# Attention scores over all 128 rows of TensorE, in smaller steps, in a hybrid decoder layer

## The chip, the cores and the metric

One core of a Trainium2 chip runs the whole layer. The metric is the device time of one execution in microseconds (us). The core has a matrix engine, TensorE (PE in the profile; PEld is its load of weights, which runs beside it), a vector engine (DVE), a scalar engine (ACT), GpSimd (POOL), and a queue SP that only issues DMA transfers. TensorE's clock has two levels, 1.2 and 2.4 GHz; the profile gives the granted clock as a share of 2.4 GHz.

## The reference, cut to what matters

One sequence of 512 tokens of width 1024, float32. The layer runs two kinds of attention on one projection, adds both through one output matrix, and then runs a feed-forward part and a gated embedding.

```
h = rmsnorm(x);  mq, mk, mv, rq, rk, rv, rg = split(h @ w_in)
# MoBA: 8 heads of 64; with 2 blocks of 256 keys and top-3 every earlier block is taken
s = (mq @ mk.T) * 64**-0.5 - slope[head] * distance      # causal
moba = softmax(s) @ mv
ret = groupnorm(chunkwise_retention(rq, rk, rv)) * silu(rg)   # 4 heads of 128
x = x + concat(moba, ret) @ w_out
h = rmsnorm(x);  x = x + (gelu(conv(h @ w_up)) * (h @ w_gate)) @ w_down
x = x + (p @ w_ple) * sigmoid(rmsnorm(x) @ w_ple_gate);  return rmsnorm(x)
```

## The kernel before

Every matrix product is made in split precision: an operand is kept as a rounded part `hi` and a rest `lo`, and `mm3` (line 91) issues three matmuls, hi by hi, hi by lo and lo by hi. ACT makes `hi`, DVE subtracts to get `lo` (`split`, line 78). Weights arrive as tiles `wr` on SP's queue, ACT makes `wh` (line 152), and DVE or POOL makes `wl` (line 154; POOL for the projection and the output matrix). There are two buffers `wr` and three each of `wh` and `wl`. SBUF tiles of 2 KB per partition come from one heap, and TensorE's results from eight PSUM banks.

The stages are: projections and retention, then the stretch from about 158 to 273 us in which MoBA is worked off, then the sum of attention outputs with the next norm, then up, gate and down products, then the gated embedding.

In the MoBA stretch two heads (one pair `g`, the two halves of a 128-row feature tile) and one block `b` of 256 queries make a round i, eight in all. `moba_scores` (line 455) makes the scores `ms` of two query tiles and both heads. Its first matmul of a score (L466) uses the 64 rows of one head: query hi by key hi. The second (L468) uses 128 rows and makes both cross products in one: the query tile holds hi in one head's half and lo in the other half, and the key tile `mk` holds lo and hi the other way round. The softmax of a score is a custom DVE operation that adds the bias and finds the smallest (`ml`, L447), an exponential with its sum on ACT (`me`, `mt`, L450), a reciprocal (`mi`, L452) and a scaling (L453) on DVE. One round later `moba_turn` (line 483) transposes the probabilities on TensorE (`mp`) and splits them into `corner`, or `mph` and `mpl` (L497, L498). Another round later `moba_values` (line 501) multiplies them with the values (`mo`) and splits the result into `mxh` and `mxl`.

Between these pieces stand fills (line 621): the last five feature projections (`pj`, 24 matmuls of 512 columns each, lines 93 to 95), the first half of the output product (`ou`, 12 each) and the products of the embedding (`pw`, 6 each, with `wph` and `pTh`, `pTl` as operands). A round is: all scores of the round, a fill, the values, the transposes, a fill.

A query projection is split into four half pieces (two ACT copies on L369, two DVE subtractions on L370). A key projection is split into one whole `mkh`, two half subtractions (L378) and two transfers on SP that put a half of `mkh` into the other half of the tile (L377). Queries come ahead of keys in the list `feature_tiles` (line 167).

After attention, for each of eight feature rows: `x` (L671) adds the output product, `h2h` and `h2l` (L88) split the next product's operand, and `squares` (line 652) squares the row on ACT and adds it to `sqs` on DVE. `next_norm` (line 663) does the split and the squares of a row together.

TensorE's order is the program's, pinned by hand (line 823). The order on the other engines comes from a scheduler, which takes due times from its own model.

## Time and profile before

| what | value |
|---|---|
| median of 3 runs | 707.64 us (707.6 to 708.22) |
| the profiled execution | 708.11 us, of which the trace's span is 706.3 us |
| TensorE busy | 688.7 us of the span, mean granted clock 0.991 |
| DVE, ACT, POOL busy | 445.6, 284.8 and 126.9 us |

The profiled execution lies 0.47 us above the median. TensorE is busy nearly all the time, so the time lost is to be looked for in single waits, which the view of waits lists by the engine that waited, what it wanted to do, and what released it. A matmul's listed duration overlaps with the next one, so what a matmul costs is read from the distance of two starts.

### The profile page before, as it was taken

What the parts mean: (1) busy time and instruction counts of PE and PEld (TensorE: products, weight loads), DVE (VectorE), ACT (ScalarE), POOL (GpSimd) and SP (SyncE); (2) the same over time, 40 slices, a digit from 0 to 9 for tenths busy, and PEclk for the clock granted to TensorE, in tenths of its full rate; (3) what the DMA queues carried; (4) which work ended last, traced back from release to release, by engine and by line L of the source; (5) the groups of instructions that cost most, each with busy time, mean ns of one, the idle gap of its engine ahead of it and who ended that gap; (6) DMA issues with size and microseconds to landing.
All of it is one profiled execution on the core that took longest, in us unless ns stands there. A gap on an engine that the chain in (4) does not pass through costs nothing.

```text
span 706.3 us, 8382 instructions
## 1 busy us (share of the span) xinstructions
PE 688.7 (98%) x3200; PEld 568.4 (80%) x3200; DVE 445.6 (63%) x792; ACT 284.8 (40%) x463; POOL 126.9 (18%) x100
## 2 busy tenths in 40 slices
PE   8999999999989999999999999999999999999995
PEld 6888888887767888788888888888888888888884
DVE  4675677777868885676556653324555665466496
ACT  4534543335555584544334332112343343354311
POOL 6135342345535111000000000000000000000146
PEclk9999999999989999999999999999999999999998
DMA  8245224325222101133133122233332311445003
GB/s 265 101 115 143 66 75 113 81 67 172 56 79 75 60 2 59 61 120 119 60 119 106 59 89 90 89 107 117 119 94 85 120 54 59 134 135 186 1 0 120
DMA packets 70525, 66.65 MB, mean 94 GB/s; under 512 B 1890, under 2 KB 62166, under 8 KB 70486
## 3 DMA queue, kind: packets, MB, share of 16 engines
q1 hardware_dynamic: 70310, 65.86, 30.2%
q8 instruction: 25, 0.41, 0.2%
q10 hardware_dynamic: 144, 0.26, 0.1%
q14 instruction: 14, 0.11, 0.0%
q0 software_dynamic: 32, 0.00, 0.0%
HBM read 62.97 MB, written 2.10 MB: 92 GB/s over the span
## 4 chain that ended last, share of the span: by engine, by line
PE 88%; DVE 7%; issue 2%; ACT 2%; DMA 0%; DVEq 0%; POOL 0%; ACTq 0%; POOLq 0%
PE gate L93 6%; PE gate L95 6%; PE dn L94 6%; PE dn L95 6%; PE gate L94 6%; PE dn L93 6%; PE up L94 5%; PE up L95 5%; PE up L93 5%; PE pj L93 5%; PE pj L94 5%; PE pj L95 5%; PE pg L94 1%; PE pg L95 1%; PE pg L93 1%
## 5 line engine op out<-in xcount | busy, mean ns | idle before, releaser
L152 ACT ACTIVATE wh<-wr 128x1024 fp32r<-128x1024 f32 (+2 forms) x108 | 105.3, 978 | 202.9 <-PE dn L94 66.4
L154 DVE TENSOR_TENSOR wl<-wr,wh 128x1024 fp32r<-128x1024 f32 (+2 forms) x78 | 84.7, 1086 | 47.8 <-ACT wh L152 47.7
L154 POOL TENSOR_TENSOR wl<-wr,wh 128x1024 fp32r<-128x1024 f32 x30 | 73.1, 2437 | 160.0 <-ACT wh L152 151.2
L94 PE MATMUL up<-h2l,wh 128*128 128x512 f32 x176 | 68.6, 390 | 1.5 <-DVE h2l L88 1.5
L93 PE MATMUL gate<-h2h,wh 128*128 128x512 f32 x176 | 68.7, 390 | 0.0
L95 PE MATMUL up<-h2h,wl 128*128 128x512 f32 x176 | 68.5, 389 | 0.0
L95 PE MATMUL gate<-h2h,wl 128*128 128x512 f32 x176 | 68.5, 389 | 0.0
L94 PE MATMUL gate<-h2l,wh 128*128 128x512 f32 x176 | 68.5, 389 | 0.0
L93 PE MATMUL up<-h2h,wh 128*128 128x512 f32 x176 | 68.5, 389 | 0.0
L93 PE MATMUL dn<-ach,wh 128*128 128x512 f32 x176 | 68.5, 389 | 0.0
L94 PE MATMUL dn<-acl,wh 128*128 128x512 f32 x176 | 68.5, 389 | 0.0
L95 PE MATMUL dn<-ach,wl 128*128 128x512 f32 x176 | 68.5, 389 | 0.0
L93 PE MATMUL pj<-h1h,wh 128*128 128x512 f32 x160 | 64.1, 401 | 2.9 <-DVE mpl L498 2.8
L94 PE MATMUL pj<-h1l,wh 128*128 128x512 f32 x160 | 63.1, 394 | 0.0
L95 PE MATMUL pj<-h1h,wl 128*128 128x512 f32 x160 | 62.9, 393 | 0.0
L691 POOL MEMSET u<- 128x2 f32 x22 | 2.2, 102 | 292.4 <-DVE c L698 292.4
L702 DVE TENSOR_TENSOR ga<-gate,r2b 128x512 f32<-128x512 f32 x22 | 15.2, 691 | 41.4 <-PE gate L95 41.4
L94 PEld LDWEIGHTS up<-h2l,wh 128*128 128x128 f32 x176 | 33.0, 188 | 8.8 <-DVE h2l L88 1.9
L692 DVE TENSOR_TENSOR u<-up,r2b 128x512 f32<-128x512 f32 x22 | 15.1, 692 | 39.3 <-PE up L95 39.3
L93 PEld LDWEIGHTS dn<-ach,wh 128*128 128x128 f32 x176 | 33.0, 188 | 6.9
L94 PEld LDWEIGHTS dn<-acl,wh 128*128 128x128 f32 x176 | 33.0, 188 | 6.9
L94 PEld LDWEIGHTS gate<-h2l,wh 128*128 128x128 f32 x176 | 33.0, 188 | 6.9
(233 smaller groups left out, 1421.9 us busy)
## 6 DMA issues: line engine op xcount, KB each, us to landing
wr<-in_w_up_dram SPq DMA_DIRECT2D x11, 1024.0 KB, 5.4
wr<-in_w_gate_dram SPq DMA_DIRECT2D x11, 1024.0 KB, 5.3
wr<-in_w_in_dram SPq DMA_DIRECT2D x20, 512.0 KB, 4.0
wr<-in_w_down_dram SPq DMA_DIRECT2D x8, 768.0 KB, 4.3
wr<-in_w_down_dram SPq DMA_DIRECT2D x8, 640.0 KB, 4.0
wr<-in_w_ple_gate_dram SPq DMA_DIRECT2D x4, 1024.0 KB, 5.6
wr<-in_w_out_dram SPq DMA_DIRECT2D x3, 1024.0 KB, 5.0
xn<-in_x_dram SPq DMA_DIRECT2D x8, 256.0 KB, 5.8
```

The lines of the kernel that those rows point to most:

```text
L93: nc.tensor.matmul(acc, a[0], b[0], start=first, stop=False)
L94: nc.tensor.matmul(acc, a[0], b[1], start=False, stop=False)
L95: nc.tensor.matmul(acc, a[1], b[0], start=False, stop=last)
L152: nc.scalar.activation(hi, part, AF.Copy)
L154: (nc.gpsimd if aside else nc.vector).tensor_tensor(lo, part, f(hi), op=ALU.subtract)
L691: nc.gpsimd.memset(u[:, 0:2], 0.0)
L692: nc.vector.tensor_tensor(u[:, 2:], up, r2b, op=ALU.mult)
L702: nc.vector.tensor_tensor(ga, gate, r2b, op=ALU.mult)
```

## The change

For each pair of heads the queries are split whole (one ACT copy, one DVE subtraction), and four transfers on SP stack hi over lo for each head in a tile `mq2`. The keys are split whole as well, and eight transfers build four tiles `mk2`: hi over hi and lo over lo for each head. A score is then two matmuls over 128 rows, the stack by hi, hi and the stack by lo, lo. This adds the product of lo by lo, which was not computed before. The number of score matmuls stays 64. The key projections come ahead of the query projections. A round's scores are cut into two steps, one query tile each, and its transposes into two, one head each, and the fills are spread over three places in a round. Last, the squares of all eight rows of `x` come after the last row's split, not with each row.

```diff
-    feature_tiles += [(n, h) for h in range(HR) for n in ("mq", "mk")]
+    feature_tiles += [(n, h) for h in range(HR) for n in ("mk", "mq")]
...
-            two = [h2k("mq", F32R) for _ in range(2)]
+            both = split(t, "mq")
+            two = [h2k("mq2", F32R) for _ in range(2)]
             for e in range(2):
-                nc.scalar.activation(two[e][HALF[e]], t[HALF[e]], AF.Copy)
-                nc.vector.tensor_tensor(two[e][HALF[1 - e]], t[HALF[e]], f(two[e][HALF[e]]), op=ALU.subtract)
+                for part, half in zip(both, HALF):
+                    nc.sync.dma_start(f(two[e][half]), f(part[HALF[e]]))
...
-            hi = hi_of(t, "mk")
-            two = [h2k("mk", F32R) for _ in range(2)]
-            for e in range(2):
-                nc.sync.dma_start(f(two[e][HALF[1 - e]]), f(hi[HALF[e]]))
-                nc.vector.tensor_tensor(two[e][HALF[e]], t[HALF[e]], f(hi[HALF[e]]), op=ALU.subtract)
-            qs[name, i] = (hi, two)
+            both = split(t, "mk")
+            two = [[h2k("mk2", F32R) for _ in range(2)] for _ in range(2)]
+            for part, tiles in zip(both, two):
+                for e in range(2):
+                    for half in HALF:
+                        nc.sync.dma_start(f(tiles[e][half]), f(part[HALF[e]]))
+            qs[name, i] = two
...
-        for qt in (2 * b, 2 * b + 1):
+        for qt in (2 * b + step,):
...
             for e in range(2):
-                nc.tensor.matmul(ss[e][:, :wide], q[e][HALF[e], own], kh[HALF[e], :wide], start=True, stop=False)
-            for e in range(2):
-                nc.tensor.matmul(ss[e][:, :wide], q[e][:, own], kx[e][:, :wide], start=False, stop=True)
+                nc.tensor.matmul(ss[e][:, :wide], q[e][:, own], kh[e][:, :wide], start=True, stop=False)
+                nc.tensor.matmul(ss[e][:, :wide], q[e][:, own], kl[e][:, :wide], start=False, stop=True)
...
-    fills = []
-    for i in range(5):
-        fills += [[big[i]], mid[i - 1:i]]
-    fills += [[mid[4], few[0]], [mid[5], few[1]], [mid[6], few[2]], [mid[7], few[3]], few[4:5], few[5:6], few[6:7],
-              few[7:8], [], []]
+    fills = [[big[0]], [], []]
+    for i in range(1, 5):
+        fills += [[big[i]], mid[i - 1:i], []]
+    fills += [[mid[4], few[0]], [mid[5]], [few[1]], [mid[6], few[2]], [mid[7]], [few[3]], [few[4]], [few[5]], [],
+              [few[6]], [few[7]], [], [], [], []]
...
-        if i < HM:
-            moba_scores(i // 2, i % 2)
-        for go in fills[2 * i]:
-            go()
+        for step in range(2):
+            if i < HM:
+                moba_scores(i // 2, i % 2, step)
+            for go in fills[3 * i + step] if step == 0 else []:
+                go()
...
-        if 1 <= i <= HM:
-            moba_turn((i - 1) // 2, (i - 1) % 2)
-        for go in fills[2 * i + 1]:
-            go()
+        for e in range(2):
+            if 1 <= i <= HM:
+                moba_turn((i - 1) // 2, (i - 1) % 2, e)
+            for go in fills[3 * i + 1 + e]:
+                go()
...
-        return squares(x1[dt], sums)
...
-            sums = next_norm(dt - 1)
-    sums = next_norm(ND - 1)
+            next_norm(dt - 1)
+    next_norm(ND - 1)
+    for t in x1:
+        sums = squares(t, sums)
```

What this does to the order is shown at three places around the first scores. On TensorE, before, the first row below is the end of projection 15 (queries of the second pair), the eight `ms` rows are the first round's scores, and `pj_16` is the key projection that follows:

```order
L95 MATMUL pj_15_1543<-h1h_8_342,wl_19_1470 128x512
L466 MATMUL ms_1_1594<-mkh_1_1500,mq_1_1435 128x256
L466 MATMUL ms_2_1595<-mkh_1_1500,mq_2_1436 128x256
L468 MATMUL ms_1_1594<-mk_1_1502,mq_1_1435 128x256
L468 MATMUL ms_2_1595<-mk_2_1503,mq_2_1436 128x256
L466 MATMUL ms_3_1614<-mkh_1_1500,mq_1_1435 128x256
L466 MATMUL ms_4_1615<-mkh_1_1500,mq_2_1436 128x256
L468 MATMUL ms_3_1614<-mk_1_1502,mq_1_1435 128x256
L468 MATMUL ms_4_1615<-mk_2_1503,mq_2_1436 128x256
L93 MATMUL pj_16_1642<-h1h_1_147,wh_20_1539 128x512
```

On TensorE now (`pj_15` is now the keys and `pj_16` the queries of the second pair):

```order
L95 MATMUL pj_15_1555<-h1h_8_342,wl_19_1480 128x512
L470 MATMUL ms_1_1616<-mk2_1_1439,mq2_1_1514 128x256
L471 MATMUL ms_1_1616<-mk2_3_1441,mq2_1_1514 128x256
L470 MATMUL ms_2_1617<-mk2_2_1440,mq2_2_1515 128x256
L471 MATMUL ms_2_1617<-mk2_4_1442,mq2_2_1515 128x256
L93 MATMUL pj_16_1640<-h1h_1_147,wh_20_1551 128x512
```

The first score pair now reads four tiles `mk2` and two tiles `mq2` that transfers have put together, and the second query tile's scores (`ms_3`, `ms_4`) have moved behind the 24 matmuls of `pj_16`.

On DVE, before, at the same place (`pt_14` takes the key projection out of PSUM, `rrv` to `rry` and `rrt` are the small steps of a reciprocal square root for retention, `mk` is the keys' lo half, `mxl` the lo part of the last retention head but one):

```order
L434 TENSOR_TENSOR rt2_3_1458<-rrow_3_1459,rt1_3_1251 128x512
L82 TENSOR_TENSOR mxl_3_1467<-rt2_3_1458,mxh_3_1465 128x512
L361 SCALAR_TENSOR_TENSOR pt_14_1498<-pj_14_1473,r1b_1_558 128x512
L228 TENSOR_SCALAR rrv_4_1513<-rcs_4_1508 128x4
L233 TENSOR_SCALAR rrs_4_1515<-rrv_4_1513 128x4
L235 TENSOR_SCALAR rrf_4_1517<-rrv_4_1513 128x4
L237 TENSOR_SCALAR rry_13_1519<-rrs_4_1515 128x4
L378 TENSOR_TENSOR mk_1_1502<-pt_14_1498,mkh_1_1500 64x512
L378 TENSOR_TENSOR mk_2_1503<-pt_14_1498,mkh_1_1500 64x512
L244 TENSOR_TENSOR rrt_10_1521<-rry_13_1519 128x4
L245 TENSOR_TENSOR rrt_10_1521<-rrt_10_1521,rrf_4_1517 128x4
```

On DVE now (`pt_14` takes the query projection out of PSUM, `mql` is the queries' lo part):

```order
L436 TENSOR_TENSOR rt2_3_1468<-rrow_3_1469,rt1_3_1251 128x512
L228 TENSOR_SCALAR rrv_4_1525<-rcs_4_1520 128x4
L233 TENSOR_SCALAR rrs_4_1527<-rrv_4_1525 128x4
L235 TENSOR_SCALAR rrf_4_1529<-rrv_4_1525 128x4
L237 TENSOR_SCALAR rry_13_1531<-rrs_4_1527 128x4
L82 TENSOR_TENSOR mxl_3_1477<-rt2_3_1468,mxh_3_1475 128x512
L361 SCALAR_TENSOR_TENSOR pt_14_1508<-pj_14_1483,r1b_1_558 128x512
L244 TENSOR_TENSOR rrt_10_1533<-rry_13_1531 128x4
L245 TENSOR_TENSOR rrt_10_1533<-rrt_10_1533,rrf_4_1529 128x4
L247 SCALAR_TENSOR_TENSOR rry_14_1536<-rrt_10_1533,rry_13_1531 128x4
L244 TENSOR_TENSOR rrt_11_1538<-rry_14_1536 128x4
L82 TENSOR_TENSOR mql_1_1512<-pt_14_1508,mqh_1_1510 128x512
```

The eviction of projection 14 has moved from ahead of `rrv` to behind `rrs`, `rry` and `mxl`, and the lo part that the scores read stands four small steps further on.

On ACT, before, behind the end of projection 14 (`mkh` and `mq` are the keys' and queries' hi parts, `wh_23` the first weights of the output product, `me` the softmax's exponentials):

```order
L75 ACTIVATE mkh_1_1500<-pt_14_1498 128x512
L152 ACTIVATE wh_22_1734<-wr_11_1536 128x1024
L369 ACTIVATE mq_3_1570<-pt_15_1568 64x512
L369 ACTIVATE mq_4_1571<-pt_15_1568 64x512
L450 ACT_TABLE_LOAD
L450 ACTIVATE me_1_1592,mt_1_1602<-me_1_1592,ml_1_1600 128x128
L450 ACTIVATE me_2_1593,mt_2_1609<-me_2_1593,ml_2_1607 128x128
L152 ACTIVATE wh_23_1786<-wr_12_1732 128x1024
L450 ACTIVATE me_1_1592,mt_3_1622<-me_1_1592,ml_3_1620 128x256
L75 ACTIVATE mkh_2_1669<-pt_16_1667 128x512
```

On ACT now (`mqh` is the queries' hi part, `mkh_2` the second pair's keys):

```order
L75 ACTIVATE mxh_3_1475<-rt2_3_1468 128x512
L75 ACTIVATE mqh_1_1510<-pt_14_1508 128x512
L152 ACTIVATE wh_22_1736<-wr_11_1548 128x1024
L75 ACTIVATE mkh_2_1582<-pt_15_1580 128x512
L152 ACTIVATE wh_23_1814<-wr_12_1734 128x1024
L452 ACT_TABLE_LOAD
L452 ACTIVATE me_1_1614,mt_1_1624<-me_1_1614,ml_1_1622 128x128
L452 ACTIVATE me_2_1615,mt_2_1631<-me_2_1615,ml_2_1629 128x128
L75 ACTIVATE mqh_2_1667<-pt_16_1665 128x512
L452 ACTIVATE me_1_1614,mt_3_1685<-me_1_1614,ml_3_1683 128x256
```

`wh_23` has moved from behind the first two exponentials to a place ahead of the table load and of all of them. It goes into the buffer of `wh_20`, which `pj_16` reads to its end.

On SP's queue the first scores now have eight transfers of keys ahead of `wr_12` and four of queries behind it. The second pair's eight key transfers stand ahead of the embedding's weights and inputs (`wpr` four times, `pn` twice) and of `wr_13`, and its four query transfers behind all of these and `wr_14`. Over the four pairs the transfers rise from 8 to 48.

## Rows read from the trace of the kernel before

**Rows 1.** The page, part 1: busy us (share of the span) and instructions of each engine.

```profile
PE 688.7 (98%) x3200; PEld 568.4 (80%) x3200; DVE 445.6 (63%) x792; ACT 284.8 (40%) x463; POOL 126.9 (18%) x100
```

**Rows 2.** TensorE's waits: what waited, for what, us in total, times, longest.

```profile
PE pj L93 <- DVE mpl L498: 2.8, 1, 2.8
...
PE up L94 <- DVE h2l L88: 1.5, 1, 1.5
PE ms L466 <- DVE corner L498: 1.2, 2, 1.0
PE pw L93 <- DVE mpl L498: 1.1, 1, 1.1
```

**Rows 3.** Stretches: length, busy time (instructions) of each engine, granted clock, DMA share, GB/s.

```profile
191.00:195.40 4.40, 3.12 (x13) 1.52 (x10) 3.22 (x9) 1.78 (x4) 0.28 (x1) 1.00 0.87 269
195.40:202.20 6.80, 4.01 (x11) 2.89 (x10) 5.99 (x11) 2.65 (x7) 3.49 (x2) 0.50 0.49 155
...
213.00:240.00 27.00, 25.88 (x137) 20.72 (x137) 21.84 (x52) 15.46 (x36) 10.93 (x7) 1.00 0.17 49
```

**Rows 4.** TensorE in time, 194 to 207 us: start, duration, line, output<-inputs, [idle before].

```profile
194.91 0.83 PE L468 MATMUL ms<-mk,mq 128*128 128x512 f32 x2
198.54 0.79 PE L93 MATMUL pj<-h1h,wh 128*128 128x512 f32 x1 [2.79 <-DVE mpl L498]
...
205.82 0.28 PE L507 MATMUL mo<-corner,mv 128*128 128x256 f32 x1
...
206.89 0.28 PE L508 MATMUL mo<-corner,mv 128*128 128x256 f32 x1
```

**Rows 5.** TensorE in time, 159 to 170 us, the first pair's scores.

```profile
159.85 0.38 PE L466 MATMUL ms<-mkh,mq 64*128 64x256 f32 x2
...
161.26 0.39 PE L93 MATMUL pj<-h1h,wh 128*128 128x512 f32 x1
...
166.72 0.60 PE L255 MATMUL rrow<-ident,rry 128*128 128x128 f32 x4
167.25 0.44 PE L466 MATMUL ms<-mkh,mq 64*128 64x384 f32 x2
...
168.17 0.51 PE L466 MATMUL ms<-mkh,mq 64*128 64x512 f32 x2
...
169.18 0.40 PE L93 MATMUL pj<-h1h,wh 128*128 128x512 f32 x1
```

**Rows 6.** POOL and DVE in time, 152 to 157 us.

```profile
154.53 2.40 POOL L154 TENSOR_TENSOR wl<-wr,wh 128x1024 fp32r<-128x1024 f32 x1 [5.32 <-ACT wh L152]
153.57 0.69 DVE L361 SCALAR_TENSOR_TENSOR pt<-pj,r1b 128x512 f32<-128x512 f32 x1 [0.33 <-PE pj L95]
154.35 0.16 DVE L228 TENSOR_SCALAR rrv<-rcs 128x4 f32<-128x4 f32 x1
154.55 2.40 DVE L233 TENSOR_SCALAR rrs<-rrv 128x4 int32<-128x4 int32 x1
```

**Rows 7.** SP's two transfers of keys in time, and transfers of tile mk to landing.

```profile
155.01 1.25 SPq L377 DMA_DIRECT2D mk<-mkh  x2
...
DMA to landing us min/median/max: 2.3/2.4/2.4
```

**Rows 8.** ACT's groups, 150 to 240 us, by shape: busy us, mean ns, idle before.

```profile
L152 ACT ACTIVATE wh<-wr 128x1024 fp32r<-128x1024 f32 x10 | 10.5, 1052 | 8.7 <-PE pj L94 5.7 <-issue 2.9
...
L450 ACT ACTIVATE me<-me,ml 128x512 f32<-128x512 f32 x6 | 4.3, 718 | 3.1 <-DVE ml L447 3.0
...
L75 ACT ACTIVATE wph<-wpr 128x512 fp32r<-128x512 f32 x4 | 2.5, 631 | 0.0
```

**Rows 9.** DVE in time, 288 to 293 us, the end of the output rows.

```profile
290.47 0.68 DVE L658 TENSOR_TENSOR sqs<-sqs,sq 128x512 f32<-128x512 f32 x1
291.07 0.68 DVE L671 TENSOR_TENSOR x<-ou,x1p 128x512 f32<-128x512 f32 x1
291.67 0.73 DVE L88 SCALAR_TENSOR_TENSOR h2l<-x,vec,h2h 128x512 fp32r<-128x512 f32 x1
```

More of the change, by code (lines that the diff above doesn't have):

```diff
@@ L435, in ret_gate @@
         mix[MW // P + h] = split(t2, "mx")
-    biases, probs, probsT = {}, {}, {}
+    biases, probs, probsT, pair = {}, {}, {}, {}
     def moba_bias(h):
@@ L453, in softmax, with moba_scores @@
         nc.vector.tensor_scalar(e, e, inv, None, op0=ALU.mult)
-    def moba_scores(g, b):
-        q, (kh, kx) = qs["mq", g], qs["mk", g]
-        pr = probs[g, b] = {}
-        if b == 0:
-            both = [h2k("me") for _ in range(2)]
-        for qt in (2 * b, 2 * b + 1):
+    def moba_scores(g, b, step):
+        q, (kh, kl) = qs["mq", g], qs["mk", g]
+        if step == 0:
+            probs[g, b] = {}
+            if b == 0:
+                pair[g] = [h2k("me") for _ in range(2)]
+        pr, both = probs[g, b], pair[g]
+        for qt in (2 * b + step,):
             keys = P * (qt + 1)
@@ L474, in moba_scores @@
                 softmax(ss[e], 2 * g + e, qt, pr[e, qt])
+        if step == 0:
+            return
         if b == 1:
-            del qs["mq", g], qs["mk", g]
+            del qs["mq", g], qs["mk", g], pair[g]
             for e in range(2):
@@ L481, in moba_scores, with moba_turn @@
                 moba_bias(2 * g + 2 + e)
-    def moba_turn(g, b):
-        pr = probs.pop((g, b))
-        probsT[g, b] = []
-        for e in range(2):
+    def moba_turn(g, b, e):
+        pr = probs[g, b]
+        if e == 0:
+            probsT[g, b] = []
+        if True:
             for kp in range(b, -1, -1):
```

## The prediction

> **What bounds the kernel now.** I read the page's busy times first. TensorE is busy for 688.7 of 706.3 us [rows 1], so there are two ways to save time: fewer or shorter matmuls, or fewer of the holes in the last 2%. The view of TensorE's waits comes next, since it names the holes. Inside the code that the change touches there are four: the fifth to last projection of the MoBA stretch waits 2.8 us for `mpl`, the first `up` 1.5 us for `h2l`, scores 1.2 us for `corner`, `pw` 1.1 us for `mpl`; together 6.6 us [rows 2]. In each the matrix engine stands at a piece whose input DVE and ACT are late with.
>
> Two things come on top. First, a hole costs more than its listed wait, because the pipeline of matmuls has to fill again. Measured from start to start, the largest takes 198.54 - 194.91 = 3.63 us [rows 4], of which the two 512-column matmuls at 194.91 should take 2 x 0.227 = 0.46 us; that leaves 3.17 against the 2.8 listed, 0.35 us more. I take 0.35 for each of five holes, 1.75 us. Second, the view of stretches shows the granted clock at 0.50, the 1.2 GHz level, from 195.4 to 202.2 us, after a stretch in which TensorE was busy for only 3.12 of 4.4 us; in 213 to 240, with a shorter hole in it, it stays at 1.00 [rows 3]. The 24 matmuls of that projection take 205.82 - 198.54 = 7.28 us [rows 4], those of an earlier one at full clock 166.72 - 161.26 = 5.46 us [rows 5]. The loss is 1.82 us. So the old holes cost 6.6 + 1.75 + 1.82 = 10.2 us in all, and this is the most that smoother order can give back.
>
> **Scores over 128 rows.** Per pair of heads the list has eight matmuls of 256 columns ahead of 161.26, from 159.85: 1.41 us. Four of 384 columns take 168.17 - 167.25 = 0.92 us, four of 512 take 169.18 - 168.17 = 1.01 us [rows 5]. At full rows I price 256 columns by the value products, 206.89 - 205.82 = 1.07 us for nine distances, 0.12 each [rows 4], and 512 by the projections, 5.46/24 = 0.227 [rows 5]; 384 columns lie between, 0.17. The same matmuls would then take 0.96 + 0.68 + 0.91 = 2.55 instead of 3.34 us, 0.79 less, and for four pairs **-3.2 us**. The number of matmuls doesn't change; what goes is the change between 64 and 128 rows, which today costs about as much as it saves. Finer steps bring more boundaries between kinds of matmul (scores, transposes, projections); I charge 16 of them 0.04 each, **+0.6 us**, between 0.2 and 1.6 (the 0.1 of a whole short matmul each).
>
> The Trainium skill speaks against this term. "TensorE: Matmul & The Clock Gate", section "Part 3: Packing small matmuls — row/col tiling", says that matmuls placed on different row groups run at the same time in the array, so that a pair over 64 rows costs about one matmul. The rows show that the two 64-row matmuls of a score pair do run together: two of them together take 0.38 us, where one 512-column matmul alone is listed with 0.39 [rows 5], so they start almost at once. The rows also show that the whole group of eight is nevertheless dearer than eight full ones, which decides for me. By the rule alone full rows would add one matmul per pair; this is a rival below.
>
> **The first scores: a new wait.** Before, the keys are split on DVE and ACT, their two transfers are issued from 155.01 on in 1.25 us and land 2.4 us after issue [rows 7], in time for 159.85. Now the last thing made is the queries, and all of their rows go through transfers. DVE meets `rrs` ahead of them, an operation of 128x4 that takes 2.40 us because POOL's `wl` of 2.40 us runs at the same time, 154.53 to 156.93 [rows 6]. Before, the eviction `pt` stood ahead of it at 153.57; now it stands behind it, with `rry` (some 0.2) and `mxl` (0.7) between. So: `rrs` ends 156.95, `rry` 157.2, `mxl` 157.9, `pt` 158.5 (0.69, [rows 6]), `mqh` 159.2 on ACT (0.63, as the other whole copy of this shape [rows 8]); then the lo part behind four small steps (0.16 to 0.2 each [rows 6]) at 159.95. SP issues at 159.2, 159.75, 160.3, 160.85 (1.25/2 each, or a little less), and the third and fourth land 2.4 us later, at 162.7 and 163.25. TensorE is ready at 159.85: 2.85 us for the first head, 0.3 more for the second, **+3.15 us**. Bounds: 2.5 if `rrs` slips ahead of POOL, 3.7 if the transfers wait for the weights `wr_12` ahead of them. The 24 matmuls of `pj_16`, then at hand, can't be taken ahead, because TensorE's order is pinned.
>
> Does that wait drop the clock? It is as long as the one at 195.4, and TensorE is busy before it; I take the measured price, **+1.82 us**, with zero as the other end. Where the clock holds, the second pair's four query transfers, which now stand behind 3 MB of weights on SP's queue, come late by up to 0.9 us, so zero is not quite reached.
>
> **The other transfers.** 40 more of 128 KB are 5 MB, on a core whose DMA share is 0.17 in 213 to 240 us [rows 3]. They hide behind that, except at the first scores and, in part, the second. SP has nothing else there that TensorE waits for.
>
> **Less on ACT and DVE.** Per pair one ACT copy (0.63 [rows 8]) and two DVE subtractions (0.69, taken as the eviction of [rows 6]) go, over four pairs 2.5 us on ACT and 5.5 us on DVE. Neither engine bounds; what it brings is in the next term.
>
> **Old holes and new ones.** With scores, transposes and fills interleaved, TensorE has work between a score and its transpose, and the old holes in the MoBA stretch lose their cause: of the 10.2 us 8.5 lie there. In their place the new order brings DVE and ACT to the limit at other points. The clearest: at the end of `pj_18` ACT takes `wh` (1.05) ahead of `wph` (0.63) and the exponential `me_6` (0.72), 2.40 us [rows 8], and reciprocal and scaling follow on DVE, some 0.3 us, while TensorE has 4 scores, 8 value matmuls and 7 transposes, 12 x 0.12 + 7 x 0.1 = 2.1 us. That leaves a hole of 0.65. I find seven places of this kind (the second `ou`, the fourteenth score, `pj_19`, `pj_20`, the fifth `ou`, the first `pw`, the first values of the third pair) and take 0.65 for each, **+4.6 us**, an estimate; ends 2.4 (every second one hidden) and 7 (each 1.0, as the longest wait of a score today [rows 2]).
>
> **Squares late.** At 290.47 DVE adds a square, 0.68 us, ahead of the addition at 291.07 and of the `h2l` at 291.67 for which TensorE waits [rows 9]. Without the eight squares DVE's queue is some 0.6 us shorter per row, the last split ends at about 289.7, and TensorE asks for it at 290.85: the whole hole, 1.5 + 0.2, goes. It is part of the 10.2 us. The sums themselves, seven of 0.6 us, end at about 293.2, and TensorE needs them some 29 matmuls after 290.85, at 297.4; if that cover of 4 us were gone, they would cost what they cost now.
>
> **The sum.** -3.2 + 0.6 + 3.15 + 1.82 - 10.2 + 4.6 = -3.2 us. On the profiled execution, 708.11, that is 704.9; on the median, 0.47 lower, **704.4 us**.
>
> **Rivals.** *The clock holds.* The first wait is a single one, and shorter holes left the clock at 1.00 [rows 3]. Then 1.82 goes from the sum and up to 0.9 comes back: 702.6 to 703.5; with the small holes at their lower end, 2.4, it is 700.4. For it: DVE has 5.5 us less to do; against it: the length, 3.15 us, like that of the one hole that did drop the clock.
>
> *A second drop (slower).* `wh_23` now stands ahead of the first exponentials on ACT and waits for the end of `pj_16`, so the first softmax starts a whole projection, 5.46 us [rows 5], later than it could. If DVE and ACT don't catch that up by `pj_19`, TensorE idles there as it did from 191 to 195.4, where 1.28 of 4.4 us were lost [rows 3] and the clock went. Price: another 1.82, small holes at 7 instead of 4.6, the first wait at 3.7: +4.8, or 709.2. [...] Against it: the two steps put a projection between first and second scores, which is time for DVE as well.
>
> *Scores don't get cheaper.* If a 64-row pair is one matmul's worth, full rows add one per pair, for one pair of heads 4 x 0.12 + 2 x 0.17 + 2 x 0.227 = 1.3 us less the 0.6 us or so of switching that goes: +0.65, for four +2.6 instead of -3.2, and 710.2. Only the sums in [rows 5] speak against it, strongly.
>
> *A wash.* The new holes take 7 us and the first wait 3.7, clock lost: 704.4 + 2.4 + 0.55 = 707.4. It is the same mechanism at its upper ends.
>
> **How the numbers follow.** A measurement of this kernel tells 0.2%, 1.4 us, from no change, so the same is 706.2 to 709.05. Chances: the forecast between 702.2 and 706.2, 0.47; the clock holds, 0.20, all faster; a wash, 0.16; a second drop 0.13 and dearer scores 0.04, both counted slower. Faster 0.67, same 0.16, slower 0.17. The range takes all of the forecast and the wash, the most of the first rival, and leaves out the two slower ones in the main: 700.8 to 708.8.
>
> **What would show it.** TensorE's first `ms` starting at 162 to 163.5 with a wait on DMA named; the clock at 0.5 in a stretch behind it and no longer at 195 to 202; the eight 256-column scores of a pair at some 0.12 each (0.24 for a pair) and not more; no wait of `up` for `h2l`; the other waits of TensorE in 165 to 260 us short and many. The prediction is wrong if the transfers' wait is under 1 us or over 4, if full-row scores still take 0.17 per 256 columns, or if one wait over 2 us stands behind 175 us.

## The result, and the profile after

The changed kernel takes 703.1 us (median of 5 runs, 701.51 to 704.48), the kernel before 707.6 (5 runs); the ratio is 0.9937, 95% interval 0.9921 to 0.9953. That is 3.3 to 5.6 us less, 4.5 by the medians; forecast were 3.2 less, 704.4 us. The profiled execution, the slowest of the five, took 704.48 us with a span of 702.6, against 708.11 and 706.3 before. The two spans differ by 3.7 us, and 0.7 of that lies ahead of 74 us, where both programs are the same and single executions scatter; 3.0 us come from what the change touches. The rest of the 4.5 us is not in this trace.

So the start of the projection `pj_14` lies anywhere from 145.75 to 148.66 us over all runs below. To compare kernels without that scatter I use two stretches of TensorE, from start to start: A, from the first matmul of `pj_14`, the fourteenth projection (the expectations below call it the fifteenth), to the first `up` matmul; and B, the first 48 `up` matmuls. A is 138.73 us before and 137.53 now. B is 24.97 and 23.18.

TensorE's waits in the changed kernel, in the columns of [rows 2]:

```profile
PE ms L470 <- DMA mq<-mql: 2.7, 1, 2.7
...
PE ms L470 <- DVE mkl L82: 1.2, 1, 1.2
PE pj L93 <- DVE corner L504: 1.1, 2, 0.8
PE ou L93 <- DVE ml L449: 0.7, 2, 0.4
PE pw L93 <- DVE corner L504: 0.7, 1, 0.7
```

The waits of [rows 2] are gone, `up` for `h2l` among them. In their place there is one long one, of the first scores for the queries' transfers, one of 1.2 us at the second pair's scores, and five under 1 us. (The view puts the 1.2 us down to `mkl`; this is the third pair's, which these scores don't read, and with the queries' transfers landing earlier, in experiment 9, the wait is gone.) TensorE in time around the first scores (answers to [rows 5]):

```profile
158.80 0.39 PE L95 MATMUL pj<-h1h,wl 128*128 128x512 f32 x1
161.86 0.39 PE L470 MATMUL ms<-mk,mq 128*128 128x256 f32 x1 [2.68 <-DMA mq<-mql]
162.09 0.28 PE L471 MATMUL ms<-mk,mq 128*128 128x256 f32 x1
162.54 0.35 PE L470 MATMUL ms<-mk,mq 128*128 128x256 f32 x1 [0.17 <-PE ms L471]
...
169.94 0.28 PE L470 MATMUL ms<-mk,mq 128*128 128x256 f32 x1
170.06 0.28 PE L471 MATMUL ms<-mk,mq 128*128 128x256 f32 x1
170.18 0.28 PE L470 MATMUL ms<-mk,mq 128*128 128x256 f32 x1
170.29 0.28 PE L471 MATMUL ms<-mk,mq 128*128 128x256 f32 x1
170.41 0.60 PE L255 MATMUL rrow<-ident,rry 128*128 128x128 f32 x4
```

From 158.80 + 0.23 to 161.86 the first head waits, 2.84 us, the second 0.34 more at 162.09. Four full-row scores of 256 columns then take 0.47 us, from 169.94 to 170.41; they were 0.705 in [rows 5]. The view of stretches (columns as in [rows 3]):

```profile
158.00:181.00 23.00, 20.15 (x89) 16.30 (x88) 11.45 (x37) 10.04 (x20) 13.31 (x7) 0.93 0.87 224
181.00:198.50 17.50, 14.93 (x80) 12.04 (x79) 10.91 (x36) 9.34 (x24) 8.32 (x6) 1.00 0.56 148
198.50:213.00 14.50, 14.18 (x77) 12.06 (x76) 10.08 (x23) 7.68 (x18) 5.12 (x3) 1.00 0.47 137
```

The granted clock is below 1 in the first stretch only, so the 1.2 GHz level has moved from behind 195 us [rows 3] to behind the first scores. And DVE around `rrs` (answers to [rows 6]):

```profile
153.81 2.40 DVE L233 TENSOR_SCALAR rrs<-rrv 128x4 int32<-128x4 int32 x1
...
156.93 0.68 DVE L361 SCALAR_TENSOR_TENSOR pt<-pj,r1b 128x512 f32<-128x512 f32 x1
...
158.31 0.69 DVE L82 TENSOR_TENSOR mql<-pt,mqh 128x512 fp32r<-128x512 f32 x1
```

### The profile page after: what moved, and what is told of

Same layout as the page of the kernel before. It is cut to its first block, busy times and chain, and to the rows that moved or that the text cites. A ratio compares the mean times of both kernels' runs of the same rounds, so it can differ in the third digit from the quotient of the medians.

```text
span 702.6 us, 8467 instructions
## 1 busy us (share of the span) xinstructions
PE 685.4 (98%) x3200; PEld 569.5 (81%) x3200; DVE 433.5 (62%) x784; ACT 282.7 (40%) x459; POOL 125.4 (18%) x100
## 4 chain that ended last, share of the span: by engine, by line
PE 89%; DVE 6%; ACT 2%; DMA 2%; issue 1%; POOL 0%; SPq 0%; DVEq 0%; ACTq 0%
PE gate L93 6%; PE gate L95 6%; PE dn L95 6%; PE up L95 6%; PE up L93 6%; PE dn L93 6%; PE gate L94 6%; PE dn L94 6%; PE up L94 6%; PE pj L93 5%; PE pj L94 5%; PE pj L95 4%; PE ou L93 2%; PE ou L94 2%; PE ou L95 2%
## 5 line engine op out<-in xcount | busy, mean ns | idle before, releaser
L95 PEld LDWEIGHTS gate<-h2h,wl 128*128 128x128 f32 x176 | 33.0, 188 | 6.9
```

The costliest lines, as they stand in the source:

```text
L95: nc.tensor.matmul(acc, a[1], b[0], start=False, stop=last)
```

## The experiments

**1. Squares late, alone.** The kernel before with this edit:

```diff
-        return squares(x1[dt], sums)
...
-            sums = next_norm(dt - 1)
-    sums = next_norm(ND - 1)
+            next_norm(dt - 1)
+    next_norm(ND - 1)
+    for t in x1:
+        sums = squares(t, sums)
```

> The kernel before, with only the squares moved behind the last split. Theory: the single hole of the first up product (wait 1.5 us for h2l, 1.7 from start to start) goes and nothing takes its place, since TensorE needs the sum of squares about 4 us after it is done: 1.7 us less than before, ratio 0.9976, no wait of up for h2l in the trace. Rival: the run of seven sums in a row delays the weights' lo parts or the sum itself, and the hole comes back at the column sums of the norm: ratio 1.000.

705.68 us (707.64 before), ratio 0.9965 (0.9952 to 0.9977). B fell from 24.97 to 23.18 us, as in the changed kernel, and TensorE has no wait left there. That is 1.8 us, and by stretch B it is the part of the gain that is surest. A is 0.7 longer than before, 139.43, because the 24 matmuls behind 195 us, in part at half clock, took 7.91 us in that execution and 7.28 before.

**2. The splits and scores of before in the new steps.**

```diff
-    feature_tiles += [(n, h) for h in range(HR) for n in ("mk", "mq")]
+    feature_tiles += [(n, h) for h in range(HR) for n in ("mq", "mk")]
...
-                nc.tensor.matmul(ss[e][:, :wide], q[e][:, own], kh[e][:, :wide], start=True, stop=False)
-                nc.tensor.matmul(ss[e][:, :wide], q[e][:, own], kl[e][:, :wide], start=False, stop=True)
+                nc.tensor.matmul(ss[e][:, :wide], q[e][HALF[e], own], kh[HALF[e], :wide], start=True, stop=False)
+            for e in range(2):
+                nc.tensor.matmul(ss[e][:, :wide], q[e][:, own], kl[e][:, :wide], start=False, stop=True)
```

(and `project` for "mq" and "mk" as before)

> The changed kernel with the splits and the score matmuls of before (four half pieces of the queries, 64-row hi product and 128-row cross product, queries ahead of keys); finer steps, fills and late squares stay. Theory: the first scores no longer wait for transfers (3.2 us) and the clock does not fall behind them (1.6 us); the scores get dearer by 2.3 us and the small holes stay within 1 us of what they are: 2.5 us faster than the changed kernel, about 700.6 us, ratio to before 0.990. Rival: the eight more DVE operations and four more ACT copies bring the holes back: 703 us or more, ratio 0.994 or above; then the transfers of the queries pay for themselves.

703.77 us, ratio 0.9946 (0.9932 to 0.996): the rival's number, although A is 136.27, 1.3 less than in the changed kernel. The first scores don't wait, but TensorE then does this:

```profile
190.82 0.60 PE L573 MATMUL pt<-ident,pn 128*128 128x128 f32 x4
193.45 0.91 PE L468 MATMUL ms<-mkh,mq 64*128 64x384 f32 x2 [2.03 <-DVE ml L447]
...
195.57 0.79 PE L93 MATMUL pj<-h1h,wh 128*128 128x512 f32 x1 [0.67 <-DVE mt L521]
```

and the 24 matmuls behind it take 7.03 instead of 5.46 us. So the first wait and its half clock are exchanged for a hole of 2.2 us (0.8 more follow) and the half clock at 195. The scores themselves, where nothing holds them: 0.65 us for four of 256 columns, 0.83 for 384, 1.00 for 512, against 0.47, 0.72 and 0.91 in the changed kernel; per pair of heads 2 x 0.18 + 0.11 + 0.09 = 0.56 us, 2.2 in all. One more cost stands ahead of each group:

```profile
159.43 0.39 PE L95 MATMUL pj<-h1h,wl 128*128 128x512 f32 x1
159.75 0.38 PE L468 MATMUL ms<-mkh,mq 64*128 64x256 f32 x2
```

Ahead of a group that begins with 64 rows the last full matmul takes 0.32 us to the next start, ahead of full-row scores 0.23 (the same pair of rows in the changed kernel). Over 16 groups that is 1.4 us. Full rows are thus cheaper by about 3.7 us.

**3. The sixteenth projection first.**

```diff
-    fills = [[big[0]], [], []]
+    big[0]()
+    fills = [[], [], []]
```

> The changed kernel with the sixteenth projection ahead of the first scores instead of behind them, so that its 5.46 us cover the queries' transfers. Theory: the wait of 3.2 us and the clock's 1.6 us go and little takes their place: 4 to 5 us faster than the changed kernel, 698.1 to 699.1 us, ratio to before 0.987; no stretch at half clock between 158 and 170 us. Rival: the scores of two query tiles now follow each other without work between them, the first softmax is as late as before, and holes of 2 to 5 us come up at the first transposes and scores of the second pair: 701 to 703 us, ratio 0.991 to 0.994.

707.41 us, ratio 0.9984 (0.9967 to 1.0002), slower than the changed kernel and than either number; A is 139.54. The rival named the places and about the size of the holes (at the first transposes 1.15 us are listed, at the second pair's scores 3.67):

```profile
178.99 0.49 PE L501 MATMUL mp<-ident,me 128*128 128x128 f32 x3
183.15 0.55 PE L470 MATMUL ms<-mk,mq 128*128 128x256 f32 x1 [3.67 <-DMA mq<-mql]
```

The first scores don't wait. The second pair's wait 3.7 us and start at 183.15. Counted from the start of `pj_14` that is 34.5 us; in the changed kernel it is 35.6. Of what was saved at 159 us, 4.8 us, only 1.1 are left by then; something else sets that time. Behind it the clock falls twice, which the rival left out: the 24 matmuls of `pj_18` and `pj_19` take 6.36 and 7.17 us, in the changed kernel 5.47 and 5.58.

**4. Scores over 64 rows only.** All four matmuls use one head's half of the rows, so that half of each score's terms is missing.

```diff
-                nc.tensor.matmul(ss[e][:, :wide], q[e][:, own], kh[e][:, :wide], start=True, stop=False)
-                nc.tensor.matmul(ss[e][:, :wide], q[e][:, own], kl[e][:, :wide], start=False, stop=True)
+                nc.tensor.matmul(ss[e][:, :wide], q[e][HALF[e], own], kh[e][HALF[e], :wide], start=True, stop=False)
+            for e in range(2):
+                nc.tensor.matmul(ss[e][:, :wide], q[e][HALF[e], own], kl[e][HALF[e], :wide], start=False, stop=True)
```

> The changed kernel with all four score matmuls of a query tile over 64 rows, head by head on the two halves of the array, so that no full-row matmul stands between them; this leaves out part of each score. Theory of the change of rows: two 64-row matmuls on different halves run at once, and what made such a pair dear before was going from 64 to 128 rows and back, so four of 256 columns take about 0.24 us from start to start plus 0.1 to 0.2 at the ends, and the 512-column ones 0.46 plus that. Rival: a 64-row matmul takes its own time whatever stands beside it: 0.48 and 0.91 us as with full rows.

```profile
177.66 0.50 PE L470 MATMUL ms<-mk,mq 64*128 64x512 f32 x2
178.00 0.40 PE L472 MATMUL ms<-mk,mq 64*128 64x512 f32 x2
178.33 0.55 PE L502 MATMUL mp<-ident,me 128*128 128x128 f32 x3
```

The one execution took 704.68 us. A pair of 64-row matmuls of 512 columns takes 0.33 us to the next start, between one full matmul (0.227) and two (0.455). Four of 256 columns take 0.43 us (0.47 with full rows). The two of a pair do run together, as the first theory says; they start 3 ns apart. What a pair takes beyond one full matmul is about 0.1 us at every width (0.22, 0.28 and 0.33 us at 256, 384 and 512 columns, against 0.12, 0.18 and 0.23); why, no run shows. Ahead of the group 0.09 us are lost here too, and behind it, at the next matmul, 0.05 to 0.1, so that at 256 columns even this form is no cheaper than full rows. With full-row matmuls in between, as in experiment 2, four cost 0.65. So the dearer part of the old scores was going from 64 to 128 rows and back.

**5. Queries split by ACT and DVE again,** scores still over 128 rows:

```diff
-            both = split(t, "mq")
-            two = [h2k("mq2", F32R) for _ in range(2)]
+            two = [h2k("mq", F32R) for _ in range(2)]
             for e in range(2):
-                for part, half in zip(both, HALF):
-                    nc.sync.dma_start(f(two[e][half]), f(part[HALF[e]]))
+                nc.scalar.activation(two[e][HALF[e]], t[HALF[e]], AF.Copy)
+                nc.vector.tensor_tensor(two[e][HALF[1 - e]], t[HALF[e]], f(two[e][HALF[e]]), op=ALU.subtract)
```

> The changed kernel with the queries split as before, in four half pieces by ACT and DVE, which write the stack of hi over lo directly; scores stay over 128 rows, keys still go through transfers, and the 16 query transfers are gone. Theory (the transfers of the queries are what costs): the first scores wait under 1 us instead of 3.2, the clock stays up (1.6 us), the second pair's scores don't wait for transfers (1.7 us), some 0.5 us come back in small holes: 5 us less between the fifteenth projection and the first up product than in the changed kernel, 698 to 699 us, ratio to before 0.987. Rival: the extra half pieces on DVE and ACT open holes of the same size later, as happened with the scores of before in the same steps: 702 to 704 us, ratio 0.993 or above.

707.65 us, ratio 1.0005 (0.9995 to 1.0015), A 141.19: my theory fell, and the rival's figure was too small too. The first wait is down to 0.6 us and the clock stays up there, as expected. Then TensorE has a hole of 3.96 us and starts the second head's scores of the second pair at 182.52. Counted from the start of `pj_14` that is 35.1 us, as in experiment 3; in the changed kernel it is 36.3. Two lines show what sets the time, ACT and TensorE:

```profile
180.16 1.06 ACT L152 ACTIVATE wh<-wr 128x1024 fp32r<-128x1024 f32 x1 [5.61 <-DMA wr<-in_w_in_dram]
...
182.52 0.58 PE L469 MATMUL ms<-mk,mq 128*128 128x256 f32 x1 [3.80 <-DVE ml L448]
```

ACT works its queue in order. `wh_24`, the weights of `pj_19`, stands ahead of the exponentials and waits 5.61 us for its transfer; the softmaxes stand still behind it, `ml` can't be formed, and, as I read the wait for it, no PSUM bank comes free for the next scores. SP's queue of the same kernel tells why the transfer is late:

```profile
164.88 2.38 SPq L379 DMA_DIRECT2D mk<-mkh  x4
167.39 2.70 SPq L379 DMA_DIRECT2D mk<-mkl  x4
170.20 1.96 SPq L563 DMA_DIRECT2D wpr<-in_w_ple_dram  x4
172.26 0.89 SPq L566 DMA_DIRECT2D pn<-in_p_dram  x2
173.25 1.23 SPq L115 DMA_DIRECT2D wr<-in_w_in_dram  x2
```

Eight key transfers take 5 us to issue, 1.5 MB for the embedding come next, and then the weights. In the changed kernel the same eight began at 161.15 and the weights were issued at 169.52. Behind the hole the clock falls (columns as in [rows 3]):

```profile
183.00:190.00 7.00, 7.00 (x22) 5.56 (x22) 5.54 (x14) 2.50 (x7) 1.95 (x2) 0.65 0.55 127
```

and once more behind waits at 197 to 200 us: the 24 matmuls of `pj_18` take 7.82 us, those of `pj_19` 7.22, in the changed kernel 5.47 and 5.58. That is most of what makes A longer than in the changed kernel; up to the start of `pj_18` this kernel is 0.9 us ahead of it.

**6 and 7. The query transfers on ACT's queue,** without and with the sixteenth projection first (`nc.scalar.dma_start` in place of `nc.sync.dma_start` for the queries).

> The changed kernel with the query transfers issued from ACT's queue instead of SP's. Theory: the second pair's scores wait 1.7 us because their transfers stand behind 1.5 MB of weights on SP's queue; on a queue of their own they land 2.3 us after issue and that wait goes, while the first wait of 3.2 us and the clock stay, and ACT is held some 0.5 us per issue: 0 to 1.5 us faster than the changed kernel, ratio to before 0.992 to 0.994. Rival: the transfers share the same engines whichever queue issues them, and land as late: same as the changed kernel or slower by the issue time on ACT, ratio 0.994 to 0.998.

> The sixteenth projection ahead of the first scores, and the query transfers on ACT's queue. In the kernel with the first edit alone the second pair's scores waited 3.9 us for query transfers behind weights. Theory: on another queue they land in time, that wait and the clock's loss behind it go (4.8 us), and nothing holds the first scores: 699 to 702 us, ratio 0.988 to 0.992. Rival: they still land late, or the projection's place itself is bad: 705 us or more.

711.6 us (ratio 1.007, 1.0043 to 1.0097) and 714.2 (1.0103, 1.0084 to 1.0122); A is 145.01 and 147.31. The first is worse than every number named for it; the second falls under its rival, 705 us or more. An issue on ACT takes 0.47 to 0.6 us, and it waits in ACT's order for DVE's lo part. The third to fifth longest of ACT's waits in experiment 6, from 155 to 190 us, in the columns of [rows 2]:

```profile
ACT me L452 <- DMA pn<-in_p_dram: 2.6, 1, 2.6
ACT wh L152 <- DMA mq<-mqh: 2.6, 1, 2.6
ACT wh L152 <- DMA wr<-in_w_in_dram: 1.9, 1, 1.9
```

Exponentials and weights now stand behind transfers too. And the transfers themselves land no sooner, as the rival said: the second pair's last two, issued on ACT at 174.20 and 175.03, land 7.9 and 7.6 us later, 35.8 and 36.4 us behind the start of `pj_14`. In the changed kernel they land 6.1 and 5.8 us after issue, 35.8 and 36.1 us behind that start.

**8. Queries by ACT and DVE, and the sixteenth projection first.**

> Queries split by ACT and DVE as before, scores over 128 rows, and the sixteenth projection ahead of the first scores. Theory: with the query transfers gone, the projection's place costs only what the late first softmax costs, 1.3 us at the first transposes and 2 to 3.5 at the second pair's later scores with a half-clock stretch: 700 to 702 us, slower than the kernel with the queries by engines alone. Rival: the wait that is left at the first scores is worth more than that, and this kernel is the faster one: under 698 us.

708.37 us, ratio 1.0006 (0.9997 to 1.0015), A 141.12: no better and no worse than experiment 5. The first scores don't wait at all, and the hole ahead of the second pair's scores grows from 3.96 to 5.79 us. `pj_18` and `pj_19` take 7.55 and 7.19 us. It is the same end, reached from a third side.

**9. The embedding's load later.** The changed kernel, with the 1.5 MB behind the first round:

```diff
-    ple_load()
...
         if i == 0:
             ret_gate(HR - 1)
+            ple_load()
```

> The changed kernel with the load of the embedding's weights and inputs (1.5 MB) placed behind the first round, so that on SP's queue it follows the weights of the nineteenth and twentieth projection and the second pair's query transfers. Theory (SP's queue sets when weights and transfers land): the second pair's queries land before 180 us and the wait of 1.7 us at 181.3 goes; the first wait and its half clock stay: 1.7 to 2.5 us faster than the changed kernel in the stretch from the fifteenth projection to the first up product (137.5), about 701 us, ratio to before 0.991. Rival: something else on ACT or DVE sets that time, and the hole only gets another name: same as the changed kernel.

703.77 us, ratio 0.9933 (0.9917 to 0.995), A 137.37 (137.53): the rival. The wait at the second pair's scores is gone, and the hole has got another name, at the next round's transposes:

```profile
189.16 0.28 PE L514 MATMUL mo<-corner,mv 128*128 128x256 f32 x1
191.71 0.98 PE L501 MATMUL mp<-ident,me 128*128 128x128 f32 x7 [2.27 <-DVE me L455]
```

**10. Experiment 5 with the embedding's load later.**

> Queries split by ACT and DVE as before, scores over 128 rows, and the embedding's load behind the first round. With the queries by engines alone, ACT waited 5.6 us for the weights of the nineteenth projection, which SP had issued only at 173.3 behind eight key transfers and 1.5 MB of embedding, and the exponentials stood behind that. Theory: now those weights are issued 3 us earlier and land 4 to 5 us earlier, the hole of 4.0 us at 178.4 and the half clock behind it (1.6 to 1.8 us) go: 5 to 6 us less than 141.2 from the fifteenth projection to the first up product, 702 to 703 us, ratio 0.993. Rival: the hole comes from the number of half pieces on DVE and ACT: 706 us or more, ratio 0.998 or above.

706.29 us, the rival's number; the ratio, 0.9963 (0.9949 to 0.9978), lies between the two. ACT's wait for the weights is down from 5.61 to 1.30 us, so SP's queue was its cause, and A falls from 141.19 to 138.59, by 2.6 instead of 5 to 6. The rest went into the same hole of 2.43 us ahead of the same transposes, at 187.5, and into a wait of 2.0 us ahead of `pj_19`, with the clock down behind it (7.07 us for its 24 matmuls).

**11. Experiment 9, with one lo part made by DVE instead of POOL** (`wl_21`, of `pj_17`):

```diff
-and key not in (("mv", 0), ("mv", 1))
+and key not in (("mv", 0), ("mv", 1), ("mk", 2))
```

> As the changed kernel with the embedding's load behind the first round, and the lo part of the eighteenth projection's weights, 2.40 us on POOL at 153.8, made by DVE instead. Theory: the operation of DVE that ran beside it no longer takes 2.40 us; with 1.1 to 1.2 us for the lo part in its place the queries are split some 1.1 us earlier, the first wait falls from 3.2 to about 2 us, and with a shorter wait the clock may hold: 1.1 to 2.7 us less than with the embedding's place alone, 698.5 to 700 us, ratio 0.988 to 0.990. Rival: DVE's own load sets the time, and the first wait stays at 3 us: no gain over the embedding's place alone.

701.87 us, ratio 0.9911 (0.9894 to 0.9929), A 136.84. On DVE:

```profile
153.02 1.23 DVE L154 TENSOR_TENSOR wl<-wr,wh 128x1024 fp32r<-128x1024 f32 x1
154.16 0.16 DVE L233 TENSOR_SCALAR rrs<-rrv 128x4 int32<-128x4 int32 x1
```

`rrs` takes 0.16 us instead of 2.40: it was long because POOL's `wl` ran. (The three earlier `rrs` of the same execution, each beside a `wl` on POOL, still take 2.37 to 2.40.) (The expectation speaks of the eighteenth projection's weights; they are the seventeenth's.) The first wait falls from 3.2 to 1.9 us, as expected. The clock falls all the same, and of the 1.3 us only 0.5 are left in A. The reason stands on ACT and, behind it, on DVE:

```profile
185.31 1.06 ACT L152 ACTIVATE wh<-wr 128x1024 fp32r<-128x1024 f32 x1 [4.75 <-issue]
186.27 0.71 ACT L452 ACTIVATE me<-me,ml 128x512 f32<-128x512 f32 x1
```

```profile
181.81 0.09 DVE L449 DVE_READ_ACCUMULATOR2_ANT ml<- 128x1 f32 x1
187.10 0.16 DVE L454 RECIPROCAL mi<-mt 128x1 f32<-128x1 f32 x1 [5.21 <-ACT me L452]
```

The minimum for `me_5` is ready at 181.9. Its exponential stands behind `wh_25`, which is for `pj_20` and goes into the buffer that `pj_18` reads to its end, at 185.3. ACT and DVE both idle for 5 us while TensorE runs `pj_18`, and then TensorE waits 2.26 us for probabilities.

**12. Experiment 11, with `wh_25` behind the last query tile's exponential.** One edge more in ACT's order, the 25th `wh` behind the eighth exponential:

```diff
+    exps, after_exp = [], {25: 8}
...
                 nc.scalar.activation(hi, part, AF.Copy)
+                if n_of['wh'] in after_exp:
+                    tc.add_manual_dep(last_of(mybir.EngineType.Activation), exps[after_exp[n_of['wh']] - 1].name, mybir.DependencyInfo(
+                        mybir.DependencyClass.NoSync, mybir.DependencyReason.DATA), reason="exponential first")
...
         nc.scalar.activation(e, e, AF.Exp, bias=least, scale=-1.0, accum_out=total)
+        exps.append(last_of(mybir.EngineType.Activation))
```

> The kernel with the embedding's load later and one lo part on DVE, and one more edge in ACT's order: the weights wh_25, needed only by the twentieth projection, stand behind the exponentials of the first pair's last query tile instead of ahead of them. In the kernel without this edge ACT stood idle for 4.75 us until the eighteenth projection had freed wh_25's buffer, DVE for 5.21 us behind it, and TensorE then waited 2.4 us for probabilities, 0.6 in transposes, 1.0 at half clock. Theory (the weights' place in ACT's order is what bounds the stretch, so earlier savings were given back there): these 4 us go and at most 1 comes back: the stretch from the fifteenth projection to the first up product falls from 136.8 to 133 to 134 us, about 698 us, ratio to before 0.985 to 0.987. Rival: the softmax is bound by its own work on DVE and ACT, the hole moves on to the next transposes: 136 us or more, ratio 0.990 or above.

697.82 us (707.6 before), ratio 0.9874 (0.9857 to 0.989). A is 131.62, 5.2 less than in experiment 11, more than expected. The hole at the transposes is gone, 4.1 us with its half clock:

```profile
184.35 0.29 PE L519 MATMUL mo<-corner,mv 128*128 128x256 f32 x1
184.48 0.93 PE L506 MATMUL mp<-ident,me 128*128 128x128 f32 x7
```

and the clock did not fall behind the first wait either, though that wait is as long as in experiment 11. This kernel beats both: 9.8 us less than the kernel before, 5.3 less than the changed one, the last a difference of medians and no paired ratio (the two ratios give 4.5).

## Why the prediction came out right, point by point

**Scores, -3.2 + 0.6.** Right in kind, and too small: -3.7 instead of -2.6 (experiment 2). The forecast left out the 0.09 us ahead of each 64-row group, and the 0.6 for finer boundaries didn't come: ahead of full-row scores a projection's matmul takes its 0.23 us. The rival that 64-row pairs are cheaper by running together is half true (experiment 4: the time of one matmul and 0.1 us for two), and changing rows costs more than that saves. On the Trainium skill's rule in "Part 3: Packing small matmuls — row/col tiling" of "TensorE: Matmul & The Clock Gate" that such a pair takes the time of about one matmul, the trace agrees in kind, the two start 3 ns apart, and not in size: the next start comes 0.1 us later than behind one matmul.

**The first wait, +3.15.** Right: 2.84 + 0.34 = 3.18. Since the whole program ran 0.74 us earlier here, the forecast's `pt` would end at 157.8, its `mql` at 159.2 and the first scores start at 162.0; measured are 157.6, 159.0 and 161.86. (The sign that was named, a start at 162 to 163.5, holds with the 0.74 us added.) `rrs` is held by POOL, as experiment 11 shows by taking POOL's work away.

**The clock behind it, +1.82.** Right: the 24 matmuls of `pj_16` take 7.08 us, 1.63 more. But the reason given, the wait's length, does not decide it. In experiments 11 and 12 the same wait of 1.5 us plus 0.3 to 0.4 stood at the same place:

```profile
160.00:168.00 8.00, 7.80 (x29) 6.17 (x29) 2.68 (x3) 0.06 (x1) 5.20 (x3) 0.79 0.73 178
```

```profile
160.00:168.00 8.00, 8.00 (x42) 6.92 (x43) 2.09 (x3) 2.29 (x2) 5.78 (x4) 1.00 0.80 202
```

The first row is of experiment 11, the second of 12: granted clock 0.79 and 1.00. Nor does the kernel: of the six executions of experiment 11, three have a mean granted clock of 0.997, as all five of experiment 12 have, in whose trace the clock is 1.00 throughout from 158 to 240 us; the other three, the traced one among them, have 0.993 to 0.995. The longer wait doesn't decide it either. Experiment 6 has the wait of the changed kernel at this place, 2.71 us listed and 0.21 more, and its clock stays at 1.00 from 160 to 168 us: the 24 matmuls of `pj_16` take 5.48 us. When the level falls after such a wait I can't tell from these runs; that the forecast met it was in part luck.

**Old holes, -10.2.** From start to start they were 10.7 us. That of the squares is gone, as experiment 1 shows; of the others two places still wait, shorter: `pj_19` (called the fifth to last projection in the prediction; it is the last but one) 0.8 us instead of 2.8, the first `pw` 0.7 instead of 1.1; both are counted below. The reason given, the interleaved steps, is not shown: experiment 2 has these steps and still a hole of 2.2 and 0.8 us at this place, with the clock down behind it. Which other part of the change closes it, no run separates.

**New holes, +4.6.** The sum of those that the list of waits shows is near, 4.98 us from start to start, the list right only in part. The second `ou` has the 0.64 that was worked out for it, and `pj_19` (0.93), `pj_20` (0.48), the fifth `ou` (0.40) and the first `pw` (0.84) are where they were said to be. The largest, 1.69 us at the second pair's scores, was given only to the case in which the clock holds; it came with the clock lost, since transfers behind 3 MB of weights, the embedding's 1.5 MB among them, landed 6 us after issue. The fourteenth score and the third pair's values have none. The two misses cancel. With the small delays between scores and the slower first matmul behind a hole it is some 6 us.

**The sum** is right in its kinds of terms: 3.0 us of 3.7 lie in what is touched, 1.8 of them in stretch B and 1.2 in A, where the forecast had 1.7 and 1.5. That it comes so close is partly luck. The scores brought 1.1 us more than forecast and the new holes cost over 1 us more, and the two cancel; the measured terms add up to -3.6, so that 0.6 us stay unaccounted for.

**What the terms don't mean.** I read them as prices: that the kernel without the first wait would be 3.2 to 5 us faster. That is false. Experiments 3, 5 and 8 take that wait away in two ways, and all are slower than the changed kernel. Counted from the start of `pj_14`, the second head's scores of the second pair start at 35.1 to 35.3 us each time, in the changed kernel at 36.3: of the wait and the clock behind it, 4.8 us together, 1.0 to 1.2 are left. Behind that point they lose 3.0 to 4.6 us against the changed kernel, most of it in `pj_18` and `pj_19`, where the clock is down. Behind the matrix engine run two queues that work in order: SP's, with twelve transfers of queries and keys and 1.5 MB of embedding ahead of the next weights, and ACT's, where a copy of weights that waits, for a transfer or for a buffer, holds the exponentials. `wh_23` ahead of the first softmax was named as a rival's mechanism; the one whose move showed in the time was its brother `wh_25` (experiment 12). In the changed kernel `wh_25` holds ACT for 4.47 us as well, and TensorE loses only the 0.64 us of the second `ou` there; once the waits ahead of it are shorter, it is the next to be met. Experiment 2 fits: the old splits reach nearly the same time, since they meet a hole of their own at 191 us, 2.2 us for `ml`, though no run shows which work in the queues holds that one.

What stays open: how much of the 5.2 us of experiment 12 is the edge alone, since experiment 12's clock also held at the first wait (1.65 us of it). The three executions of experiment 11 with the same mean clock took 700.2 to 701.53 us, median 700.58, against 697.82; by that the edge is worth 2 to 3 us, an estimate, as the two were measured at different times and the kernel before moved by 0.65 us between them. The edge on the changed kernel, without the edits of experiments 9 and 11, was not run.

## What to carry to other kernels

A hole on the bounding engine is a price only if nothing behind it is as late. Before you sum up what a wait costs, look at the next place where the engine stops, and ask whether its cause would start any earlier. In a queue that works in order, look for an instruction that waits for something far ahead of those that are needed now: on ACT a copy for the next but one projection held the softmax for 5 us, and one edge in the order, on top of two smaller moves, made the kernel some 5 us faster again. And compare starts between kernels from a common point of the program: the times here shifted by up to 2.9 us between executions ahead of anything that the runs differ in. And transfers put between engines to save vector work cost issue time (0.6 us each here) on a queue that also brings the weights.

## What the runs showed of the hardware

A DVE operation on 128x4 int32 numbers took 2.40 us beside POOL's 128x1024 subtraction and 0.16 us without it. Two 64-row matmuls on different halves started 3 ns apart and took 0.33 us to the next start for 512 columns, not 0.227 and not 0.455; a pair cost about 0.1 us beyond one full matmul at 256, 384 and 512 columns alike. The full-row matmul ahead of such a pair took 0.32 instead of 0.23 us. Transfers of 128 KB landed 2.3 us after issue ahead of the first scores, and behind the embedding and weights of 3 MB, which SP had issued, 6 us after issue from SP's queue and 8 from ACT's. The clock fell to its lower level behind a wait of 1.9 us in one kernel and stayed up behind the same wait in another; behind 3 us it fell in the changed kernel and stayed up in experiment 6. Executions of one kernel differed in it too (mean granted clock 0.993 to 0.997).
